# A hybrid GLA and RetNet decoder step: the input projection computed once for all tokens with seven products in place of eight, and spilled to DRAM

## The chip, the cores and the metric

The kernel runs on one core of a Trainium2 chip. The metric is device time in microseconds (us) of one execution. TensorE (PE) multiplies matrices, VectorE (DVE), ScalarE (ACT) and GpSimd (POOL) work elementwise, SyncE (SP) issues most transfers. Each engine runs its own instructions in order and waits on semaphores.

## The reference

One layer, for 1024 prompt tokens and 8 x 4 sample tokens (8 sequences that continue from stored states). All arithmetic is fp32.

```python
shift, scale, gate = split(c @ w_ada + b_ada)
h = x * (1 + scale) + shift
p = h @ w_in                      # 1024 -> 11280 columns
# GLA: q, k (4 heads x 128), v, z (4 x 256), low-rank forget input (16)
# RetNet: q, k (4 x 256), v, z (4 x 512); two merge gates of 1024
GLA:    S_t = diag(alpha_t) S_{t-1} + k_t^T v_t ; o_t = q_t S_t ; RMSNorm, * silu(z)
RetNet: rotary on q, k; S_t = gamma_h S_{t-1} + k_t^T v_t ; o_t = q_t S_t ; GroupNorm, * silu(z)
merged = sigmoid(mg) * (o_g @ w_branch_gla) + sigmoid(mr) * (o_r @ w_branch_ret)
y = LayerNorm(alpha * x + gate * (merged @ w_out))
```

Outputs are y and the final states of both branches, for prompt and sample.

## The kernel before, in words

**Precision.** A product of two fp32 matrices is made of three matmuls in the faster fp32r type: each operand is split into a high part (ScalarE copy, `split` L114, `wunit` L109) and a low part (VectorE subtraction, L115, L110), and hi x hi, lo x hi and hi x lo are summed in PSUM. So every block of 128 x 128 weights costs three matmuls. `wunit` loads 512 KB of weights and splits them.

**Halves.** The tokens are worked in two halves, `half(0)` with 512 prompt tokens and the 32 sample tokens, `half(1)` with the other 512. Each half runs the whole layer: `prep` makes h with channels on partitions, `ret_phase` goes through the four RetNet heads, `gla_phase` through the four GLA heads, `merge_phase` through the branches and gates, and the output projection and LayerNorm follow. All weights are read and split once in each half. States pass from half to half through DRAM.

**Projection.** `w_in` is not projected as a stage. Each head projects its own q and k (`proj_T`, `mm3`, L214 to L216: channels on PSUM partitions, 256, 288 or 512 tokens per matmul), its v (`v_units`, L246 to L248 and L253: tokens on partitions, 256 channels per matmul) and its z (`z_proj`), just before it needs them. `MR` and `MG` project the merge gates.

**Attention.** Both branches run in chunks of 128 tokens, four in each half. `A0` makes the masked scores of all chunks (L325, L664), `CPa`, `CPv` and `CP` split a chunk's operands, `C(c)` makes its output and updates the state S (L420, L738), `norm` normalises (with `rsqrt` on POOL, L124 and L125), `G(c)` transposes (L277), multiplies with silu(z) and splits. For sample tokens `ld(b)` or `SB` loads a stored state, `spl` splits it, `smm` multiplies and updates, and the new state is stored (L456, L471, L473, L475). `B(ob)` multiplies a head's result with the RetNet branch weights (L507 to L509) and adds into `acc`; `BG` does so for GLA (L850 to L852). `out_blk` is the output projection (L899 to L901).

**Order.** The order is written out by hand: `ret_phase` and `gla_phase` build a list `main`, in which the chunks of one head alternate with its z projections, the branch units of the head before, and q, k, v of the next head; `weave` spreads the sample units over it by the units' costs. The instructions of an engine are finally ordered when the program is built, by its own plan and not only in the order of this text.

Of the kernel before, what the change touches and what calls it, by code (L numbers as in the profile page):

```python
# [18 lines left out]
P = 128  # L19
# [4 lines left out]
NCH = 4  # L24
# [7 lines left out]
SUBOFF = (0, 32, 96, 192)  # L32


@with_exitstack
def hybrid_step(ctx: ExitStack, tc: tile.TileContext, a: dict):
# [21 lines left out]
    fold = ctile("fold", [64, 9], eng=nc.sync)  # L58
# [3 lines left out]
    def load_consts():  # L62
        rmask_s = ctile("rmask_s", [NS, HEADS, NS], eng=nc.sync)
        repsr = ctile("repsr", [P, HEADS], eng=nc.sync)
        repsr_s = ctile("repsr_s", [NS, HEADS], eng=nc.sync)
        rdw = ctile("rdw", [P, HEADS], eng=nc.sync)
        rdw_s = ctile("rdw_s", [NS, HEADS], eng=nc.sync)
        bmask_q = ctile("bmask_q", [P, 8, NS], eng=nc.sync)
        bmask_k = ctile("bmask_k", [P, 8], eng=nc.sync)
        scanm = ctile("scanm", [P, P + NS], eng=nc.sync)  # L70
        rg = ctile("rg", [P, 16], eng=nc.sync)
        gg = ctile("gg", [P, 8], eng=nc.sync)
        blr2 = ctile("blr2", [P, HEADS], eng=nc.sync)
        CC.__dict__.update(locals())

    def load_gmask():
        CC.gmask = const.tile([P, P], U8, name="gmask")
        CC.gmask_s = const.tile([NS, NS], U8, name="gmask_s")
        mtmp = wk.tile([P, 2, P], F32, tag="S0", name="mtmp", bufs=1)
        nc.gpsimd.dma_start(mtmp[:, 0, :], a["gmask"])  # L80
        nc.gpsimd.dma_start(mtmp[:NS, 1, :NS], a["gmask_s"])
        nc.vector.tensor_copy(CC.gmask, mtmp[:, 0, :])
        nc.vector.tensor_copy(CC.gmask_s, mtmp[:NS, 1, :NS])
# [3 lines left out]

    s_ret = [dp.tile([P, 2, DV_R], F32, name=f"sret{h}") for h in range(HEADS)]
    s_gla = [dp.tile([P, DV_G], F32, name=f"sgla{h}") for h in range(HEADS)]
    gate_d = dp.tile([2, P, 1024], F32, name="gate_d")  # L90

    def ps_mm():
        return psA.tile([P, 512], F32, tag="mm", name="mm")

    def ps_aux():
        return psA.tile([P, 512], F32, tag="aux", name="aux")

    def ps_o():
        return psC.tile([P, 512], F32, tag="o", name="o")

    def ps_so():
        return psC.tile([P, 512], F32, tag="so", name="so")

    def wunit(src, shape):
        raw = wp.tile(shape, F32, tag="raw", name="raw", bufs=2)
        nc.sync.dma_start(raw, src)
        wh = wp.tile(shape, F32R, tag="wh", name="wh")
        wl = wp.tile(shape, F32R, tag="wl", name="wl")
        nc.scalar.activation(wh, raw, AF.Copy)  # L109
        nc.vector.tensor_tensor(wl, raw, wh.bitcast(F32), op=sub)  # L110
        return wh, wl

    def split(hi, lo, src):
        nc.scalar.activation(hi, src, AF.Copy)  # L114
        nc.vector.tensor_tensor(lo, src, hi.bitcast(F32), op=sub)  # L115

    mhalf = const.tile([P, 1], F32, name="mhalf")
    nc.gpsimd.memset(mhalf, -0.5)

# [7 lines left out]
    def c_stack(t):  # L127
        nc.vector.tensor_scalar(t.rearrange("p k c -> p (k c)"), ident[:, 0:1].to_broadcast([P, KB * 64]), 0.0, None,
                                op0=mult)
        nc.scalar.activation(t[:, :, 0:9], cT, AF.Copy)  # L130
        nc.vector.tensor_tensor(t[:, :, 32:41], cT, t[:, :, 0:9].bitcast(F32), op=sub)
        return t

    def ada_fin(ps, kb):
        t = wk.tile([64, 256], F32, tag="on", name="mod", bufs=3)
        nc.scalar.activation(t, ps[:64, :256], AF.Copy)
        pt = ps[:, 256:274].rearrange("p (w c) -> p w c", w=2)
        for which in range(2):
            nc.tensor.matmul(pt[:, which, :], t[:, which * P:(which + 1) * P], fold, start=True, stop=True)
        nc.vector.tensor_tensor(modT[:, kb], pt, bada[:, :, kb:kb + 1].to_broadcast([P, 2, 9]), op=add)  # L140

    def gate_units(vj):
        Gt = SimpleNamespace()

        def begin():
            Gt.cT = c_stack(vj[:, 0, :].rearrange("p (k c) -> p k c", k=KB))
            Gt.sel = wk.tile([9, P + NS], F32, tag="rm", name="sel", bufs=1)
            nc.gpsimd.dma_start(Gt.sel, a["sel"])

        def col(j, kh):  # L150
            if kh == 0:
                Gt.ps = ps_mm()
            w = wunit(a["wgate"][2 * j + kh], [P, 4, 256])
            for k in range(4):
                for i in range(2):
                    nc.tensor.matmul(Gt.ps[:64, :256], Gt.cT[:, 4 * kh + k, :], w[i][:, k, :],
                                     start=kh + k + i == 0, stop=kh + k + i == 5)
            if kh == 1:
                g = wk.tile([P, TMAX], F32, tag="th", name="gn", bufs=3)[:9, :512].rearrange("p (i c) -> p i c", i=2)
                nc.gpsimd.dma_start(g[:, 0], a["bgate"][:, j * 256:(j + 1) * 256].partition_broadcast(9))  # L160
                nc.scalar.activation(g[:, 1], Gt.ps[32:41, :256], AF.Copy)
                nc.vector.tensor_tensor(g[:, 0], Gt.ps[:9, :256], g[:, 0], op=add)
                nc.vector.tensor_tensor(g[:, 0], g[:, 0], g[:, 1], op=add)
                Gt.g = g

        def spread(j):
            pm = ps_mm()
            for i, (c0, n) in enumerate(((0, P), (P, NS))):
                ps = pm[:n, i * 256:(i + 1) * 256]
                nc.tensor.matmul(ps, Gt.sel[:, c0:c0 + n], Gt.g[:, 0], start=True, stop=True)  # L170
                t = wk.tile([n, 256], F32, tag="on", name="gt", bufs=3)
                nc.scalar.activation(t, ps, AF.Copy, scale=0.5)
                nc.sync.dma_start(gate_d[i, :n, j * 256:(j + 1) * 256], t)

        L = [begin]
        for j in range(4):
            L += [lambda j=j: col(j, 0), lambda j=j: col(j, 1), lambda j=j: spread(j)]
        return L

    def half(hf):  # L180
        H = SimpleNamespace()
        T = TMAX if hf == 0 else TH
        groups = ((0, 256), (256, 544)) if hf == 0 else ((0, 512),)
        sample = hf == 0
        tb = [(c * P, P) for c in range(NCH)] + ([(TH, NS)] if sample else [])
        st_ = SimpleNamespace()
# [1120 lines left out]
```

## Time and profile before

| what | value |
|---|---|
| median of 3 runs | 1786.26 us (1785.05 to 1786.39) |
| profiled execution, span | 1784.8 us |
| PE busy | 1753.9 us (98%), 11724 matmuls |
| DVE busy | 1082.4 us (61%) |
| ACT busy | 797.8 us (45%) |
| POOL busy | 227.7 us (13%) |
| moved by DMA | 209.63 MB, 117 GB/s |

The profiled execution's own time, outside the profiler's span, is not given apart; its span is 1.5 us below the median of the runs. A row of a group reads: line, engine, operation, output<-inputs, shapes, count | busy us, mean ns of one | idle time of the engine before them, and what ended it. A row of a timeline reads: start, duration, engine, line, operation. A row of windows reads: stretch, its length, then busy time and count of PE, PEld (weight load), DVE, ACT, POOL, then the granted clock, the DMA share and GB/s. A row of waits reads: who waited for whom: us in total, times, longest.

### The profile page before, as it was taken

To read this page: it belongs to the slowest core of one execution; us is meant where nothing else is said; L and a number is where in the kernel's file an instruction comes from. 1 tells how busy PE (TensorE), PEld (TensorE's weight loads), DVE (VectorE), ACT (ScalarE), POOL (GpSimd) and SP (SyncE) were. 2 spreads that over 40 slices of the span, in tenths; PEclk is the share of its full clock that TensorE was granted. 3 is DMA by queue.
4 is the path that set the end of the run, shared out by engine and by line. 5 is a ranking of instruction groups with operands and counts; after the bars stand their busy time and mean duration, and the time that the engine had idled before them with its cause. 6 is when DMAs were issued, how large, how long until landed. Compare 5 with 4: busy or idle time off the path is not lost.

```text
span 1784.8 us, 29201 instructions
## 1 busy us (share of the span) xinstructions
PE 1753.9 (98%) x11724; PEld 1597.4 (90%) x11724; DVE 1082.4 (61%) x2065; ACT 797.8 (45%) x1463; POOL 227.7 (13%) x387
## 2 busy tenths in 40 slices
PE   7999999999999999999999999999999999999997
PEld 6999999999989999999999989888898888888887
DVE  5567467676588766655447765373645765544447
ACT  6453553453456555654224353432434644444320
POOL 3112011111120112112011000010000010001001
PEclk9999999999999999999999999999999999999999
DMA  7434343434452334434244422323232222222342
GB/s 281 137 124 162 121 152 120 142 130 136 142 178 95 108 93 147 126 101 148 94 161 129 135 71 97 97 94 95 62 115 73 87 79 71 84 83 86 95 165 83
DMA packets 62120, 209.63 MB, mean 117 GB/s; under 512 B 8883, under 2 KB 9856, under 8 KB 61984
## 3 DMA queue, kind: packets, MB, share of 16 engines
q1 hardware_dynamic: 44288, 146.50, 25.5%
q0 software_dynamic: 17696, 61.27, 10.2%
q8 instruction: 92, 1.51, 0.4%
q14 instruction: 44, 0.36, 0.1%
HBM read 176.54 MB, written 31.20 MB: 116 GB/s over the span
## 4 chain that ended last, share of the span: by engine, by line
PE 89%; DVE 4%; DMA 3%; ACT 1%; POOL 1%; issue 1%; SPq 0%; POOLq 0%; DVEq 0%; ACTq 0%
PE mm L214 13%; PE mm L215 13%; PE mm L216 13%; PE mm L246 5%; PE mm L247 5%; PE mm L248 5%; PE mm L507 3%; PE mm L508 3%; PE mm L509 3%; PE o L420 3%; PE aux L420 2%; PE mm L850 2%; PE mm L851 2%; PE mm L852 2%; PE aux L664 2%; DMA xt<-xT 2%
## 5 line engine op out<-in xcount | busy, mean ns | idle before, releaser
L214 PE MATMUL mm<-hh,wh 128*128 128x256 f32 (+2 forms) x1512 | 493.7, 328 | 0.7 <-POOL hh L207 0.5
L216 PE MATMUL mm<-hh,wl 128*128 128x256 f32 (+2 forms) x1512 | 490.4, 325 | 1.3 <-DVE wl L110 1.3
L215 PE MATMUL mm<-hl,wh 128*128 128x256 f32 (+2 forms) x1512 | 490.1, 324 | 0.9 <-DVE hl L208 0.9
L110 DVE TENSOR_TENSOR wl<-raw,wh 128x1024 fp32r<-128x1024 f32 x246 | 299.3, 1220 | 255.5 <-ACT wh L109 254.3
L109 ACT ACTIVATE wh<-raw 128x1024 fp32r<-128x1024 f32 x246 | 258.5, 1057 | 391.6 <-PE mm L215 219.9
L216 PEld LDWEIGHTS mm<-hh,wl 128*128 128x128 f32 x1512 | 286.3, 189 | 25.1 <-DVE wl L110 1.5
L215 PEld LDWEIGHTS mm<-hl,wh 128*128 128x128 f32 x1512 | 286.5, 189 | 23.1 <-DVE hl L208 1.4
L214 PEld LDWEIGHTS mm<-hh,wh 128*128 128x128 f32 x1512 | 285.6, 189 | 24.0 <-POOL hh L207 0.9
L246 PE MATMUL mm<-wh,hh 128*128 128x256 f32 x768 | 218.1, 284 | 0.0
L247 PE MATMUL mm<-wl,hh 128*128 128x256 f32 x768 | 216.4, 282 | 0.0
L248 PE MATMUL mm<-wh,hl 128*128 128x256 f32 x768 | 216.0, 281 | 0.0
L246 PEld LDWEIGHTS mm<-wh,hh 128*128 128x128 f32 x768 | 145.1, 189 | 1.1
L247 PEld LDWEIGHTS mm<-wl,hh 128*128 128x128 f32 x768 | 145.2, 189 | 0.5
L248 PEld LDWEIGHTS mm<-wh,hl 128*128 128x128 f32 x768 | 145.3, 189 | 0.0
L507 PE MATMUL mm<-oh,wh 128*128 128x288 f32 (+2 forms) x384 | 123.8, 323 | 0.0
L508 PE MATMUL mm<-ol,wh 128*128 128x288 f32 (+2 forms) x384 | 123.7, 322 | 0.0
L509 PE MATMUL mm<-oh,wl 128*128 128x288 f32 (+2 forms) x384 | 123.3, 321 | 0.0
L507 PEld LDWEIGHTS mm<-oh,wh 128*128 128x128 f32 x384 | 72.2, 188 | 5.8
L508 PEld LDWEIGHTS mm<-ol,wh 128*128 128x128 f32 x384 | 72.2, 188 | 5.3
L509 PEld LDWEIGHTS mm<-oh,wl 128*128 128x128 f32 x384 | 72.2, 188 | 5.1
L473 DVE SCALAR_TENSOR_TENSOR s0p<-s0p,aux 128x512 f32<-128x512 f32 x64 | 43.6, 682 | 45.0 <-PE aux L469 44.7
L899 PE MATMUL mm<-wh,mg 128*128 128x256 f32 x224 | 63.6, 286 | 2.6 <-ACT wh L109 1.6
(346 smaller groups left out, 3132.8 us busy)
## 6 DMA issues: line engine op xcount, KB each, us to landing
raw<-wqk_r SPq DMA_DIRECT2D x32, 512.0 KB, 3.7
s0p<-state_ret POOLq DMA_DIRECT2D x32, 512.0 KB, 4.2
raw<-wv_r SPq DMA_DIRECT2D x32, 512.0 KB, 3.6
raw<-wz_r SPq DMA_DIRECT2D x32, 512.0 KB, 3.6
o_srs<-s0p POOLq DMA_DIRECT2D x32, 512.0 KB, 3.4
raw<-wb_r SPq DMA_DIRECT2D x32, 512.0 KB, 3.6
raw<-wm SPq DMA_DIRECT2D x32, 512.0 KB, 3.5
stage<-wada SPq DMA_DIRECT2D x16, 512.0 KB, 7.5
```

The lines of the kernel that those rows point to most:

```text
L109: nc.scalar.activation(wh, raw, AF.Copy)
L110: nc.vector.tensor_tensor(wl, raw, wh.bitcast(F32), op=sub)
L214: nc.tensor.matmul(ps, w[0][:, k, cols], hh[:, k, g0:g1], start=k == 0, stop=False)
L215: nc.tensor.matmul(ps, w[0][:, k, cols], hl[:, k, g0:g1], start=False, stop=False)
L216: nc.tensor.matmul(ps, w[1][:, k, cols], hh[:, k, g0:g1], start=False, stop=k == KB - 1)
L246: nc.tensor.matmul(ps[:, :256], xh, wh[:, k % 4, :], start=k == 0, stop=False)
L247: nc.tensor.matmul(ps[:, :256], xh, wl[:, k % 4, :], start=False, stop=False)
L248: nc.tensor.matmul(ps[:, :256], xl, wh[:, k % 4, :], start=False, stop=k == KB - 1)
L420: nc.tensor.matmul(out, lhs(l), rhs(r), start=start and i == 0, stop=stop and i == 2)
L507: nc.tensor.matmul(ps, wh[:, j, cols], R.oh[:, j, g0:g1], start=j == 0, stop=False)
L508: nc.tensor.matmul(ps, wh[:, j, cols], R.ol[:, j, g0:g1], start=False, stop=False)
L509: nc.tensor.matmul(ps, wl[:, j, cols], R.oh[:, j, g0:g1], start=False, stop=j == 3)
```

## The change

The program becomes two stages, `project()` and `attend()`, each with its own buffers.

**Projection.** All 1056 tokens are projected together, as two sets of 528 (`HT`: 512 prompt and 16 sample tokens). One group is 256 columns of `w_in`, and its product is taken as 2 x 2 x 2 blocks: two token sets, two halves of the 1024 channels, two blocks of 128 columns. In place of the eight block products there are seven, of sums and differences of the blocks (a Winograd form of Strassen's scheme). The seven token operands (`XH`, `XL`, high and low) are made once, by `combos`; the four weight differences of each group are made by `tsum` on POOL, and `parts` splits each of the seven weight operands of 512 elements per partition. `step` runs one product as 2 x 12 matmuls of 264 tokens, `outs` recombines from PSUM. There are 44 groups. All results, v too, now have channels on partitions.

The post work of a group (`post_copy`, `post_z`, `post_rot`, `post_gla`, `post_m`) is run in portions within the next group's steps: rotary, the GLA decay products, silu, tanh. Its results are stored to DRAM tensors.

**Attention.** `attend()` reads them back by chunks (`ld`, `ldv`), and takes all eight chunks of a head in one go, so no state passes through DRAM. Order: GLA heads 0 and 1 (`gla_pair(0)`, with the gate columns woven in), four RetNet heads (`ret_stage`, with branch units: of the GLA pair beside head 0, of head h-1 beside head h), GLA heads 2 and 3 (`gla_pair(1)`, with the branch units of RetNet head 3), then the last branch units, the output projection in blocks of 512 columns, and LayerNorm. V is transposed on TensorE in `CP` and `CPv`. Several low parts move from DVE to POOL: those of queries, of GLA scores and of sample states (`spl`, `SB`). The branch products run in three groups of 352 tokens.

The diff, cut to its core:

```diff
-    h0, h1 = half(0), half(1)
...
+        def tsum(g, i):
+            r, T = G[g].raw, G[g].T
+            t = T[i] = wp.tile([P, 512], F32, tag="T", name="T", bufs=3)
+            x, y = {1: lambda: (r[:, 0, 1], r[:, 0, 0]), 2: lambda: (r[:, 1, 1], T[1]),
+                    3: lambda: (r[:, 1, 1], r[:, 0, 1]), 4: lambda: (r[:, 1, 0], T[2])}[i]()
+            nc.gpsimd.tensor_tensor(t, x, y, op=sub)
...
+        ORDER = ("P2", "P1", "P5", "P6", "P3", "P4", "P7")
...
+            split(wh.rearrange("p j c -> p (j c)"), wl.rearrange("p j c -> p (j c)"), right(g, p))
...
+            for j in js:
+                for i, (w, x) in enumerate(((wh, xh), (wh, xl), (wl, xh))):
+                    nc.tensor.matmul(ps[:, :SUB], w[:, j, :], x[:, j, c], start=start and j == 0 and i == 0,
+                                     stop=stop and j == 3 and i == 2, skip_group_check=True)
...
+        def combos(j):
+            h0, h1 = xs[j], xs[j + 4]
+            S, S_ = st("S12"), st("S34")
...
+            nc.vector.tensor_tensor(S[:, 0], h0[:, 1], h1[:, 1], op=add)
+            sp(4, S[:, 0])
+            nc.vector.tensor_tensor(S[:, 1], S[:, 0], h0[:, 0], op=sub)
+            sp(5, S[:, 1])
...
+            emit_parts(n + AHEAD)
...
+                step(g, i)
+            for _ in range(rate[0]):
+                if todo:
+                    todo.pop(0)()
+            if i == 6:
+                while todo:
+                    todo.pop(0)()
+                todo += plan[g][2](G[g])
+                if g + 2 < NG:
+                    load_raw(g + 2)
...
+            def CPv(c):
+                v = R.vz[c][0]
+                pv = ps_aux()
+                for j in range(4):
+                    nc.tensor.transpose(pv[:, j * P:(j + 1) * P], v[:, j, :], ident)
+                vj = R.vj[c] = wk.tile([P, 2, DV_R], F32R, tag="vj", name="vj", bufs=1)
+                split(vj[:, 0], vj[:, 1], pv)
...
+            def SPl():
+                s = R.s12 = wk.tile([P, 12, NS], F32, tag="s12", name="s12")
+                for j in range(4):
+                    for o, src in ((0, qk_d), (4, v_d), (8, z_d)):
+                        nc.gpsimd.dma_start(s[:, o + j].rearrange("p (h t) -> p h t", h=2), src[h][:, j, :, TH:])
...
+            def spl(b, d):
+                R.ar = wk.tile([P, 2, DV_R], F32R, tag="ar", name="ar")
+                split(R.ar[:, 0], R.ar[:, 1], R.sb[b][0][:, d, :], nc.gpsimd)
...
+            for c in range(NCH):
+                main.append((3.4, lambda c=c: C(c)))
...
+            weave(main, samp, fill)
...
+        og0 = gla_pair(0, gate_units)
...
+            fill = branch(4, og0[0], og0[1], fin_g0)
+            for h in range(HEADS):
+                oh, ol = o4("oh"), o4("ol")
+                ret_stage(h, oh, ol, wk, fill)
+                if h < 3:
+                    fill = branch(h, oh, ol, fin_r(h))
...
+        og1 = gla_pair(1, fill_r3)
...
+    project()
+    attend()
```

More of the change, by code (lines that the diff above doesn't have):

```diff
@@ L101, in ps_so @@
[L101 to L115, printed above, removed]
+    dec = const.tile([P, HEADS, 16], F32, name="dec")
@@ L125, in rsqrt @@
         nc.gpsimd.tensor_tensor(out, out, mhalf[:n], op=ALU.pow)
[L127 to L178, printed above, removed]
@@ L390, in open_s @@
[L390 to L397 removed]
+                v = R.vz[c][0]
+                pv = ps_aux()
+                for j in range(4):
+                    nc.tensor.transpose(pv[:, j * P:(j + 1) * P], v[:, j, :], ident)
@@ new lines, in ret_stage @@
+            samp = [S0, lambda: ldb(0), lambda: ldb(1)]
+            for b in range(8):
+                for d in range(2):
+                    samp += [lambda b=b, d=d: spl(b, d), lambda b=b, d=d: smm(b, d)]
+                if b + 2 < 8:
+                    samp.append(lambda b=b: ldb(b + 2))
+            samp += [SF, SG]
+            for f in (lambda: ld(0), lambda: ldv(0), SPl, lambda: ld(1), lambda: ldv(1), lambda: A0(0), SP,
+                      lambda: CPa(0), lambda: CPv(0)):
+                f()
@@ L510, in B @@
                     if h == 0:
-                        nc.scalar.activation(st_.acc[:, ob, g0:g1], ps, AF.Copy)
+                        nc.scalar.activation(A, ps, AF.Copy)
                     else:
-                        nc.vector.tensor_tensor(st_.acc[:, ob, g0:g1], ps, st_.acc[:, ob, g0:g1], op=add)
-            R.qku = cost(5.3, [lambda w=w, g=g: qk(w, g) for w in range(2) for g in range(len(groups))])
-            R.open, R.qkf, R.A0, R.SP, R.open_v, R.open_att = open_, qk, A0, SP, open_v, open_att
@@ L929, in out_ln @@
                 nc.sync.dma_start(dst[:, cs], yh)
-        H.__dict__.update({k: v for k, v in locals().items() if callable(v)})
-        H.groups, H.tb, H.sample, H.st = groups, tb, sample, st_
-        return H
-    def cost(w, units):
-        for u in units:
-            u.w = w
-        return units
-    def weave(main, extra):
-        ws = [getattr(u, "w", 0.3) for u in main]
-        n, m, i, done = sum(ws), len(extra), 0, 0.0
-        for u, w in zip(main, ws):
+        seq = [8] + list(range(8))
@@ L944, in weave @@
+        for c in seq:
+            xld(0, c)
+        for c in seq:
+            blk(0, c)
+        xld(1, seq[0])
+        for n, c in enumerate(seq):
+            if n + 1 < 9:
+                xld(1, seq[n + 1])
+            blk(1, c)
+            ln(c)
+    def weave(main, extra, fill):
+        total = sum(w for w, _ in main) or 1.0
+        ne, nf = len(extra), len(fill)
+        ie = jf = 0
+        done = 0.0
+        for w, u in main:
             u()
             done += w
-            while i < m and (i + 1) * n <= done * m + 1e-6:
-                extra[i]()
-                i += 1
@@ L1163, in hybrid_step @@
[L1163 to L1178 removed]
+            while jf < nf and (jf + 0.5) * total <= done * nf + 1e-6:
+                fill[jf]()
+                jf += 1
@@ L1181, in _constants @@
+            while ie < ne and (ie + 1) * total <= done * ne + 1e-6:
+                extra[ie]()
+                ie += 1
+        for u in extra[ie:]:
+            u()
+        for u in fill[jf:]:
+            u()
+    project()
+    attend()
 def _constants():
```

1784 lines of the change are left out of this document (925 added, 859 removed).

## The prediction

> **What bounds the kernel now.** I read the engine shares first, then the chain that ended last, then rows of single matmuls.
>
> ```profile
> span 1784.8 us, 29201 instructions
> PE 1753.9 (98%) x11724; PEld 1597.4 (90%) x11724; DVE 1082.4 (61%) x2065; ACT 797.8 (45%) x1463; POOL 227.7 (13%) x387
> PE 89%; DVE 4%; DMA 3%; ACT 1%; POOL 1%; issue 1%; SPq 0%; POOLq 0%; DVEq 0%; ACTq 0%
> ```
>
> TensorE is busy 98% of the span and carries 89% of the chain; no other engine comes near. But a busy matmul row overlaps its neighbours, so the price of one is the distance between starts. In the timeline (start, duration, engine, line):
>
> ```profile
> 900.04 0.28 PE L214 MATMUL mm<-hh,wh 128*128 128x256 f32 x1
> ...
> 902.06 0.28 PE L216 MATMUL mm<-hh,wl 128*128 128x256 f32 x1
> 902.18 0.29 PE L214 MATMUL mm<-hh,wh 128*128 128x288 f32 x1
> ...
> 905.23 0.29 PE L216 MATMUL mm<-hh,wl 128*128 128x288 f32 x1
> ...
> 1177.89 0.39 PE L214 MATMUL mm<-hh,wh 128*128 128x512 f32 x1
> ...
> 1180.40 0.39 PE L216 MATMUL mm<-hh,wl 128*128 128x512 f32 x1
> 1180.63 0.60 PE L277 MATMUL aux<-c_ident,on 128*128 128x128 f32 x4
> 1180.99 1.64 PE L420 MATMUL aux<-vj,kn 128*128 128x512 f32 x6
> ```
>
> Between the first two rows lie 17 starts: 0.119 us for 256 columns. 23 starts in the next pair give 0.133 us for 288, 11 starts 0.228 us for 512. Interpolated: 0.122 us at 264 columns, 0.160 at 352. The price falls nearly with the columns, so fewer columns is less time. Four transposes take 0.36 us, 0.09 each.
>
> **The projection.** Groups by line and shape:
>
> ```profile
> L246 PE MATMUL mm<-wh,hh 128*128 128x256 f32 x768 | 218.1, 284 | 0.0
> L214 PE MATMUL mm<-hh,wh 128*128 128x512 f32 x512 | 205.4, 401 | 0.0
> L214 PE MATMUL mm<-hh,wh 128*128 128x288 f32 x496 | 146.4, 295 | 0.5 <-POOL hh L207 0.5
> L214 PE MATMUL mm<-hh,wh 128*128 128x256 f32 x504 | 142.5, 285 | 0.2
> L899 PE MATMUL mm<-wh,mg 128*128 128x256 f32 x224 | 63.6, 286 | 2.6 <-ACT wh L109 1.6
> ```
>
> L214 has two equal companions (L215, L216), L246 has L247 and L248. Before: 3 x (512 x 0.228 + 496 x 0.133 + 504 x 0.119) = 728 us, 2304 V matmuls x 0.119 = 274, the sample rows of V (L253, 192) 23, the first head's parts that went to other PSUM tiles (72) 9: 1034 us. After: 44 groups x 7 products x 2 halves x 12 = 7392 matmuls of 264 columns x 0.122 = 904 us. **Gain 130 us.**
>
> The other TensorE terms: out_blk in 512 columns instead of 256, 768 x 0.119 against 384 x 0.228: -4. Branches: the same columns in three groups of 352, nil. V now arrives with channels on partitions, so 216 new transposes x 0.09: +19. The forget gate's input, 80 matmuls instead of 48 (the second token set needs three terms): +2. Two more prices by the timeline:
>
> ```profile
> 14.59 0.61 PE L139 MATMUL aux<-c_fold,mod 64*128 64x9 f32 x4 [0.21 <-ACT mod L136]
> 649.88 3.74 PE L664 MATMUL aux<-GZ,kh 128*32 128x32 f32 x32
> ```
>
> The adaLN matmuls become 128 plain fp32 of 9 columns, each two rows (as L139's two matmuls show four): 256 x 0.15 = 38 us at most. I cost them at nothing, since they lie in the start beside some 48 us of transfers (below); with that cover gone they would add 16 us over today's 144 x 0.119 and 32 x 0.15. A0 of one head and half (L664) takes 3.7 us, as before. Net -113 us.
>
> **What covers what in the first stage.** One group is 168 x 0.122 = 20.5 us of TensorE.
>
> ```profile
> L110 DVE TENSOR_TENSOR wl<-raw,wh 128x1024 fp32r<-128x1024 f32 x246 | 299.3, 1220 | 255.5 <-ACT wh L109 254.3
> L115 DVE TENSOR_TENSOR Sx<-S,Sx 128x512 fp32r<-128x512 f32 x48 | 31.1, 686 | 2.4 <-ACT Sx L114 2.0
> L513 DVE TENSOR_TENSOR acc<-mm,acc 128x288 f32<-128x288 f32 x24 | 10.9, 455 | 10.2 <-PE mm L509 10.1
> L114 ACT ACTIVATE ar<-s0p 128x512 fp32r<-128x512 f32 x64 | 40.1, 627 | 33.0 <-DMA s0p<-state_ret 14.2 <-PE so L471 6.4 <-DVE ar L115 5.9
> L573 POOL MEMSET AT<- 128x512 f32 x2 | 1.1, 529 | 4.0 <-PE o L420 4.0
> ```
>
> Posts are priced by elements, 0.69 us for 512 on VectorE and 0.63 on ScalarE. VectorE per group: 7 weight splits x 0.69 + 8 recombinations of 264 columns x 0.43 = 8.2 us; the rotary post adds 6.7, the GLA post about 7: at most 15 of 20.5. ScalarE: 7 x 0.63 + 8 x 0.4, plus 5 in z groups: 12.6. POOL gets four subtractions of 512 (new there): one lies between 0.53 us (the memset, which only writes) and 1.6 (three such streams); I take 1.1, 4.4 us a group. Only the four GLA groups, whose post has some 16 us on POOL, come near 20.5. Nil while TensorE sets the pace; cover gone, up to 2 us in each of these four. Per group 1 MB is read and 1.1 MB spilled through SP, 102 GB/s; over the run the spill and its reading add about 115 MB and the second reading of the weights (63 MB) goes, so 210 becomes about 262 MB, 150 GB/s.
>
> ```profile
> 0.00:50.00 50.00, 39.41 (x258) 32.98 (x259) 26.35 (x34) 30.46 (x40) 18.06 (x35) 1.00 0.78 285
> 50.00:100.00 50.00, 48.29 (x393) 47.17 (x392) 28.09 (x59) 22.89 (x42) 3.24 (x9) 1.00 0.35 109
> ```
>
> The start moved 285 GB/s (last column), so 150 is nil. Its own length is bytes: w_ada 8.4 MB, both token halves 4.3, the first weights 1, at 285 GB/s 48 us, then one set of splits; before, one half (2.2) and 1.6 MB of weights: 43. **+5 us.**
>
> **What lost its cover: the attention.** Before, every chunk had projections beside it. Now GLA pair 0 has only the gate columns as fill, each RetNet head eight branch units, pair 1 eight more. In pair 0 ScalarE is the bound:
>
> ```profile
> L114 ACT ACTIVATE vjg<-GV 128x256 fp32r<-128x256 f32 x32 | 13.2, 413 | 0.3
> L114 ACT ACTIVATE xS<-AT 128x128 fp32r<-128x128 f32 x32 | 9.8, 305 | 0.0
> L719 ACT ACTIVATE on<-o,ssq 128x256 f32<-128x256 f32 x32 | 15.2, 475 | 31.9 <-POOL ssq L125 31.9
> L717 ACT ACTIVATE on<-o 128x256 f32<-128x256 f32 x32 | 12.1, 379 | 5.1 <-DMA gate_d<-gt 4.2 <-PE o L738 0.9
> L772 ACT ACTIVATE kst<-kdr,c_bmask_k 128x128 fp32r<-128x128 f32 x32 | 11.3, 393 | 2.1 <-DVE kdr L228 2.1
> L109 ACT ACTIVATE wh<-raw 128x1024 fp32r<-128x1024 f32 x246 | 258.5, 1057 | 391.6 <-PE mm L215 219.9 <-PE mm L508 66.0 <-PE mm L851 25.5
> ```
>
> A chunk costs it three splits of 256 (0.41 each), two of 128 (0.305), Square with its 0.2 read-out, and the scaled copy: 2.9 us, x 16 = 46. Samples 16 x 0.39 + 8 x 0.63 = 11, gate weights 8 x 1.06 = 8.5, the rest (set-up, A0's split) 13: 79 us. TensorE has there 16 chunks x 9 x 0.119, samples 6, A0 15, transposes 7, gates 8: 53. With ScalarE filled to 85% the pair takes 93: **+40 us**. In pair 1, with branch work, TensorE has 89 and VectorE about 90 (60 of the pair, 24 x 1.06 of the merge, 5 of weights); two engines that full seldom mesh, I take 104: **+15**. In a RetNet head TensorE has 96 us (26 chunk matmuls, 46 branch, 11 samples, the rest transposes and scores) and VectorE 90 (per chunk 6.7, per sample batch 1.6, per branch unit 2.2, by 0.69 for 512 wide and about 0.42 for 256): **+4 each, +16**. The nearest row is the window where VectorE was 85% busy and TensorE still full (nothing lost); the other bound is a tenth, 10 each:
>
> ```profile
> 550.00:600.00 50.00, 50.00 (x402) 48.84 (x401) 42.63 (x111) 31.05 (x51) 0.12 (x1) 1.00 0.28 85
> L320 POOL DMA_DIRECT2D rm<-rmask x8 | 4.6, 570 | 51.5 <-DVE Af L327 50.0 <-PE mm L170 1.6
> ```
>
> Between the stages the last group's post, its store, fresh loads of 3 to 4 us and one score and split set stand alone: **+12**. At heads' borders 12 small sample loads go through POOL (0.57 us each by the last row); branch units cover them, 7 us each where not.
>
> The sum: 1784.8 - 113 + 5 + 40 + 15 + 16 + 12 = 1760, against a span of 1784.8; the median of the runs is 1.5 above it: **1761 us**. The 80 us that TensorE was not filled before (1785 less 1705 by these prices) are left in.
>
> **A rule against the change.** The splits' low parts of queries, scores and sample states move from VectorE to POOL. In the trace POOL has almost no elementwise work (13% busy, much of it issue). The Trainium skill, GPSIMD Engine Reference, sections 3.1 and Key points, says that a two-input operation takes POOL about twice VectorE's time and that POOL contends with VectorE instructions that have two SBUF inputs; by it a 512-wide one is an estimated 1.35 us and the third rival's 1846 would be about 1865. No row here shows it.
>
> **Rivals.** (1) TensorE stays fed: units are moved across chunks. For it: the build does not keep the order of the text. In the code A0's L664 stands wholly before the first Z's L214; in the trace:
>
> ```profile
> 590.60 0.30 PE L664 MATMUL aux<-GZ,kh 128*64 128x32 f32 x2
> 590.83 0.33 PE L673 MATMUL aux<-c_ident,KE 128*128 128x128 f32 x1
> 590.91 0.37 PE L214 MATMUL mm<-hh,wh 128*128 128x256 f32 x1
> 591.12 0.28 PE L664 MATMUL aux<-GZ,kh 128*96 128x32 f32 x2
> ```
>
> Against: pair 0 has too little to move. 1784.8 - 113 + 5 + 12 + 1.5 = 1690.
>
> (2) Slower by one wait: POOL's queue in the RetNet samples. ldb's load waits until the store from that buffer has landed, and the split's low part, now on POOL, stands behind it; smm on TensorE waits for that, and behind smm the next chunk. By waits and POOL's timeline:
>
> ```profile
> POOL s0p L456 <- DMA o_srs<-s0p: 59.9, 21, 5.7
> 503.00 0.73 POOL L475 DMA_DIRECT2D o_srs<-s0p  x1 [1.16 <-DVE qp L458]
> 509.46 0.72 POOL L456 DMA_DIRECT2D s0p<-state_ret  x1 [5.72 <-DMA o_srs<-s0p]
> ```
>
> The wait exists (21 times, 2.9 us mean); before, only rsqrt stood behind it. Store, landing and load take 3 to 6.5 us and the low part 1.1: some 5 us a batch, and by the woven order 20 of 32 batches have no branch unit in between: 1761 + 100 = 1861. It decides from 25 us on, 0.8 us a batch. Against: the moved order above.
>
> (3) POOL and VectorE exclude each other: per RetNet head POOL gets 16 x 1.1 + 7 x 0.6 = 22 us, VectorE 90 + 22 = 112, so +12 each; the pairs' 19 us on top of 90 and 71 add 22 and 13: 1761 + 85 = 1846.
>
> (4) The seven products give no gain, were a start bound by its weight load; the three prices by columns speak against it.
>
> **How the numbers follow.** Less than 0.2% can't be told from no change here. Forecast 0.50, between 1722 (the uncovered terms halved) and 1790; rival 1 0.12; rival 2 0.22; rival 3 0.13; no change by mixture 0.03. The range reaches to 1700 and 1870: below lies most of rival 1, above part of rival 2. Faster 0.60 (forecast less 0.02, and rival 1), same 0.05, slower 0.35. The forecast's own range is 1722 to 1790.
>
> **What would show it.** Right: 7392 projection matmuls spaced 0.12 us, ending near 970 us; pair 0 some 90 us long with ScalarE over 80% busy; RetNet heads about 100 us with VectorE near 90%. Wrong: TensorE waiting on POOL's ar in the samples (rival 2), VectorE's 512-wide subtractions longer than 0.69 us (rival 3), or gaps in the first stage behind POOL's subtractions.

## The result, and the profile after

The changed kernel takes 1978.91 us (1972.42 to 1982.17), the kernel before beside it 1786.33: a ratio of 1.108 [1.105, 1.110], 193 us slower. The prediction said 1761 us and faster. Since e5 below shows the seven products to be worth 133 us, everything else in the change costs about 326 (193 + 133).

The page of the changed kernel: its shares, TensorE's busy time and clock in 40 slices, and the chain by engine:

```profile
span 1970.6 us, 31563 instructions
PE 1768.3 (90%) x11944; PEld 1636.0 (83%) x11944; DVE 1138.1 (58%) x2120; ACT 825.2 (42%) x1695; POOL 747.5 (38%) x899
PE   7899888999999999999997878889898997876796
PEclk9999999999999999999997779999999999897898
PE 65%; DMA 11%; POOL 10%; DVE 6%; ACT 5%; issue 4%; SPq 0%; POOLq 0%; DVEq 0%; ACTq 0%
```

TensorE falls from 98 to 90% of a longer span and from 89 to 65% of the chain. POOL's busy time triples. Cut at the borders of the stages (columns as in the windows of before):

```profile
0.00:100.00 100.00, 80.16 (x368) 76.95 (x369) 38.51 (x63) 33.15 (x52) 21.87 (x44) 1.00 0.47 163
100.00:360.00 260.00, 233.99 (x1850) 228.80 (x1849) 154.14 (x287) 133.50 (x249) 109.83 (x123) 0.97 0.34 112
360.00:1031.30 671.30, 671.30 (x5532) 671.21 (x5530) 350.23 (x575) 289.04 (x564) 196.50 (x145) 1.00 0.30 105
1031.30:1054.80 23.50, 10.97 (x62) 9.02 (x60) 8.86 (x22) 7.71 (x15) 12.79 (x20) 0.64 0.76 231
1054.80:1157.80 103.00, 84.35 (x468) 67.73 (x468) 64.80 (x160) 61.09 (x188) 61.43 (x102) 0.78 0.56 172
1157.80:1288.00 130.20, 107.81 (x562) 89.83 (x563) 87.29 (x163) 53.90 (x101) 60.22 (x75) 0.92 0.73 219
1288.00:1402.00 114.00, 105.66 (x581) 90.15 (x581) 74.37 (x140) 62.26 (x121) 57.99 (x73) 0.98 0.53 156
1402.00:1517.00 115.00, 102.50 (x567) 86.61 (x566) 80.92 (x157) 51.45 (x95) 53.91 (x68) 0.99 0.51 148
1517.00:1635.00 118.00, 107.75 (x586) 92.56 (x587) 84.07 (x166) 51.86 (x96) 53.42 (x69) 0.96 0.44 131
1635.00:1758.00 123.00, 106.53 (x705) 95.62 (x703) 82.13 (x208) 59.85 (x184) 63.33 (x107) 0.94 0.57 171
1758.00:1856.00 98.00, 60.58 (x269) 52.12 (x269) 40.94 (x74) 16.68 (x28) 30.18 (x39) 0.83 0.41 122
1856.00:1970.60 114.60, 96.73 (x412) 75.42 (x410) 71.86 (x112) 4.68 (x7) 26.08 (x41) 0.93 0.29 99
```

These are, in order: the start; the GLA groups of the projection; its other groups; the border; GLA pair 0; the four RetNet heads; pair 1; the last branch units; the output. The third row is what the change is for: 5532 matmuls in 671.30 us, 0.1213 us each, with TensorE never idle. No other row is like it.

| stage | predicted us | measured us | more |
|---|---|---|---|
| projection, start included | 970 | 1031.3 | 61 |
| border | 12 | 23.5 | 11 |
| GLA pair 0 | 93 | 103 | 10 |
| four RetNet heads | 400 | 477.2 | 77 |
| GLA pair 1 | 104 | 123 | 19 |
| last branch units and output (what is left of 1760) | 181 | 212.6 | 32 |
| sum | 1760 | 1970.6 | 210 |

TensorE's waits from the border to the output (who waits for whom: us in total, times, longest) name four places:

```profile
PE mm L661 <- DVE thl L1208: 36.2, 20, 4.3
PE aux L996 <- ACT on L960: 15.1, 4, 4.0
PE so L1060 <- POOL ar L93: 14.4, 20, 1.3
PE mm L1122 <- DVE cstk L1112: 9.1, 1, 9.1
```

The first is the last branch units, the second the ends of the four heads, the third the sample states' low parts on POOL, the fourth the border, where the gate columns' operand is late.

### The profile page after: what moved, and what is told of

It is laid out like the page before. It is cut to its first block, busy times and chain, and to the rows that moved or that the text cites. A ratio compares the mean times of both kernels' runs of the same rounds, so it can differ in the third digit from the quotient of the medians.

```text
span 1970.6 us, 31563 instructions
## 1 busy us (share of the span) xinstructions
PE 1768.3 (90%) x11944; PEld 1636.0 (83%) x11944; DVE 1138.1 (58%) x2120; ACT 825.2 (42%) x1695; POOL 747.5 (38%) x899
## 4 chain that ended last, share of the span: by engine, by line
PE 65%; DMA 11%; POOL 10%; DVE 6%; ACT 5%; issue 4%; SPq 0%; POOLq 0%; DVEq 0%; ACTq 0%
PE psA L157 18%; PE psC L157 12%; PE psD L157 6%; PE psB L157 6%; DMA thl<-m0d 3%; PE o L647 3%; PE mm L661 2%; PE mm L662 2%; PE mm L663 2%; PE aux L647 2%; PE psada L495 2%; PE aux L709 2%; POOL ar L93 1%; POOL acc L1207 1%; POOL kh L408 1%
## 5 line engine op out<-in xcount | busy, mean ns | idle before, releaser
L157 PE MATMUL psA<-xh,wh 128*128 128x264 f32 x1056 | 301.8, 286 | 6.8 <-ACT C L193 6.8
L157 PE MATMUL psA<-xl,wh 128*128 128x264 f32 x1056 | 301.0, 285 | 0.8 <-DVE xl L93 0.8
L157 PE MATMUL psA<-xh,wl 128*128 128x264 f32 x1056 | 300.9, 285 | 0.0
L157 PE MATMUL psC<-xh,wh 128*128 128x264 f32 x704 | 202.2, 288 | 9.7 <-ACT xh L92 7.0
L157 PEld LDWEIGHTS psA<-xh,wh 128*128 128x128 f32 x1056 | 199.4, 189 | 7.7 <-ACT C L193 7.6
L157 PE MATMUL psC<-xl,wh 128*128 128x264 f32 x704 | 201.3, 286 | 0.0
L157 PEld LDWEIGHTS psA<-xl,wh 128*128 128x128 f32 x1056 | 199.7, 189 | 1.7 <-DVE xl L93 1.7
L157 PE MATMUL psC<-xh,wl 128*128 128x264 f32 x704 | 201.1, 286 | 0.0
L157 PEld LDWEIGHTS psA<-xh,wl 128*128 128x128 f32 x1056 | 199.9, 189 | 0.0
L93 DVE TENSOR_TENSOR wl<-raw,wh 128x512 fp32r<-128x512 f32 (+1 forms) x164 | 144.9, 890 | 90.9 <-ACT wh L92 90.6
L157 PEld LDWEIGHTS psC<-xl,wh 128*128 128x128 f32 x704 | 133.5, 190 | 0.8 <-DVE xl L93 0.7
```

Source lines behind the costliest of these rows:

```text
L93: (eng or nc.vector).tensor_tensor(lo, src, hi.bitcast(F32), op=sub)
L157: nc.tensor.matmul(ps[:, :SUB], w[:, j, :], x[:, j, c], start=start and j == 0 and i == 0, stop=stop and j == 3 and i == 2, skip_group_che ...
```

## The experiments

Ratios are to the kernel before on the same chip, to be read against 1.108 [1.105, 1.110] of the change as it was.

### What the seven products are worth

**e5: an eighth product.** `prod` runs P3 once more into D's PSUM in each group, and P4, which belongs there, overwrites it.

```diff
                     q.b["D", s] = bank("BD", 3, "psD")
+                    prod(g, "P3", s, q.b["D", s], True, True)
```

> The changed kernel with an eighth product in each group (24 more matmuls of 264 columns into a PSUM bank that the next product overwrites; 1056 matmuls in all, outputs unchanged). It measures what the seventh part less is worth. Theory A (TensorE sets the pace of the first stage): +1056 x 0.121 = 128 us, less what the four GLA groups and the start hide, so +110 to +130, about 2095. Rival C (the seven products are paced by the splits, the recombination or POOL's differences, so that the saved product bought little): +0 to +60.

2112.46 us, ratio 1.183 [1.180, 1.186]: +133.5 for 1056 matmuls more, 0.126 us each and just above the range. The saved product is paid out in full; the loss is elsewhere.

### The start

The chain of the start, in order of time (start, length, what):

```profile
1.64 3.83 DMA ada<-wada
5.61 13.80 PE psada L495 x64
19.43 0.19 DVE modT L497
...
20.30 1.25 ACT xt L507
...
23.50 1.78 DVE xl L93
...
28.29 6.64 PE psada L495 x32
```

adaLN's rows take 13.80 / 64 = 0.216 us each, 256 of them 55 us, and each block's sums and splits stand behind its adaLN.

The 0.216 us is a slow clock, though the windows read 1.00 for this stretch. The matmuls of 264 columns that lie between the adaLN blocks start 0.22 us apart up to 95.5 us, and from there 0.12 us apart (TensorE's timeline):

```profile
94.19 0.42 PE L157 MATMUL psC<-xh,wl 128*128 128x264 f32 x1
94.42 0.42 PE L157 MATMUL psC<-xl,wh 128*128 128x264 f32 x1
...
96.82 0.28 PE L157 MATMUL psA<-xl,wh 128*128 128x264 f32 x1
96.94 0.28 PE L157 MATMUL psA<-xh,wl 128*128 128x264 f32 x1
```

Their weight loads take 0.33 us in the first part and 0.19 in the second, as they do on the two sides of the head's end shown further down, where the granted clock reads 0.50 and then 1.00. An adaLN row at the full rate stands in e10 (below), right where its matmuls of 264 columns turn from 0.22 to 0.14 us apart; eight rows take 0.95 us, 0.12 each:

```profile
21.94 0.95 PE L491 MATMUL psada<-c_cT,c_ident 128*128 128x9 f32 x8
```

**e2: adaLN with moving weights.** fp32r, 256 columns moving, hence 32 splits of w_ada on ScalarE and VectorE.

```diff
-                    nc.tensor.matmul(pt[:, w, :], raws[kb][k // 4][:, k % 4, w * P:(w + 1) * P], cT[:, k, :], ...
+                split(wh, wl, raws[kb][q // 2][:, 2 * (q % 2):2 * (q % 2) + 2, :])
...
+                        nc.tensor.matmul(ps[:64, :256], cs[:, 2 * q + k, :], w[:, k, :], ...
```

> The changed kernel, with the adaLN parameters computed as before the change: c stationary (high and low part stacked), 256 columns of weights moving, a fold, instead of 128 plain fp32 matmuls of 9 columns that need 256 weight loads. Theory A: those 256 rows stood 0.2 us apart on the path of the first 100 us; now 128 rows and 32 of the fold, so the first stage's full rate begins near 65 us instead of 98, whole about 1945. Rival B (the start is set by the 13.7 MB of transfers, as my prediction had it, 48 us plus splits): the start does not move by more than 5 us.

1972.34 us, 1.105 [1.102, 1.108]: not distinguishable from no change. VectorE's work in the first 100 us rose from 38.5 to 63.3 us, ScalarE's from 33.2 to 56.1.

From this I concluded that adaLN is not the start's limit. That was wrong, as the next runs show. Why this form gains nothing has two candidates that are not told apart: the splits of w_ada load the engines that the tokens' sums and splits need, and TensorE again runs at the slow rate up to 91.5 us, but for 51 to 64 us.

**e7: no loads of w_ada; e11: a quarter of adaLN's matmuls; e10: both.**

```diff
 e7, e10:
-                nc.sync.dma_start(r, a["wada"][2 * kb + kh])
-   ... matmul(pt[:, w, :], raws[kb][k // 4][...], cT[:, k, :]
+   ... matmul(pt[:, w, :], ident, cT[:, k, :]
 e10, e11:
-                for k in range(KB):
+                for k in (0, 4):
```

> The sixteen loads of w_ada are left out; the 128 adaLN matmuls read the identity instead, so their number and shape stay and the modulation's values differ. Theory C (the start is a chain: loads go out two at a time as the nine buffers of st come free, some 19 us a pair, and TensorE, fed in pieces, runs at half rate until 98 us): without those loads six of the ring's turns are gone, and the full rate begins near 60 us: -30 to -45 us. Rival D (the start is TensorE's and VectorE's own work, adaLN, modulation and sums in order, at half rate): -0 to -10 us.

> The loads of w_ada are left out as before and of adaLN's 128 matmuls only a quarter is left (two of eight k steps, on the identity), so the modulation's values differ. Without the loads alone the time did not move, and the chain then ran over adaLN's matmuls (0.216 us for each of 256 rows, 56 us of the first 83). Theory C2 (the start has two chains of the same length side by side, the loads and adaLN on TensorE, and taking one leaves the other): with both gone the full rate begins near 55 us, -30 to -45 us. Rival (x's loads, sums and splits hold the start): 0 to -15 us.

> The loads of w_ada stay and adaLN has a quarter of its matmuls (two of eight k steps; the values differ). Theory C2: the loads' chain is left, -5 to -15 us, as adaLN with moving weights gave -6.6. Rival (adaLN on TensorE alone is the start's chain): -30 to -45 us, as much as with the loads gone too.

e7: 1976.59 us, 1.108 [1.105, 1.111], nothing. e11: 1946.73, 1.090 [1.086, 1.094], -32. e10: 1932.17, 1.082 [1.080, 1.085], -47. In e7 theory C fell and its rival D held. e10 came out just past its range, but e11 is as its rival said, so theory C2, two chains of the same length, fell too. adaLN on TensorE is the start's chain: taking 8 MB of transfers away gains nothing while it stands, taking three quarters of it away gains 32 with all the transfers in place, and the loads are worth 15 more only behind it. In e7's chain of the first 110 us adaLN's rows have 44.1%.

**e13: e2 with the low parts on POOL.**

```diff
-                split(wh, wl, raws[kb][q // 2][:, 2 * (q % 2):2 * (q % 2) + 2, :])
+                split(wh, wl, raws[kb][q // 2][:, 2 * (q % 2):2 * (q % 2) + 2, :], nc.gpsimd)
```

> adaLN with the weights moving (fp32r, 256 columns, as in the earlier run that gave -6.6) and their low parts on POOL instead of VectorE. If VectorE's and ScalarE's splits were what that form paid with: -15 to -25 us against the changed kernel. If POOL's 1.3 to 1.45 us for each of 32 low parts (about 44 us) takes their place in the chain, or the loads hold the start: 0 to -8 us.

1979.67 us, 1.107 [1.103, 1.111]: nothing. Relieving VectorE alone does not help; the slow rate lasts up to 96.4 us here, and again the splits and the clock are not told apart.

**e14: plain fp32 with the nine columns as weights and w_ada moving, unsplit.**

```diff
+                nc.tensor.matmul(ps[:9, :256], cT[:, k, :], raws[kb][k // 4][:, k % 4, :], start=k == 0, stop=k == KB - 1)
+            nc.scalar.activation(t, ps[:9, :256], AF.Copy)
...
+                nc.tensor.matmul(pt[:, w, :], t[:, w * P:(w + 1) * P], ident[:9, :9], start=True, stop=True)
```

> adaLN in plain fp32 with the nine columns as weights and w_ada moving, 64 matmuls of 256 columns instead of 128 of nine, with no splits; the result is turned by 16 small matmuls. A plain fp32 matmul of 256 columns took some 0.6 to 1.0 us in the gate spread, two rows: 64 x 0.62 = 40 us at the better rate against 56 us. If adaLN on TensorE is the start's chain: -8 to -18 us. If the moving rows run at the worse rate (64 x 1.0 = 64 us): 0 to +8 us.

1953.90 us, 1.091 [1.089, 1.094]: -25, above the range expected. In the tile's rows (duration min/median/max in ns), the first two of the changed kernel, the others of e14:

```profile
L495 PEld LDWEIGHTS psada<-c_cT,ada x256: 285/333/337, 5.6 to 87.9; 128*128 128x128 f32 x128
L495 PE MATMUL psada<-c_cT,ada x256: 216/362/363, 5.6 to 87.9; 128*128 128x9 f32 x128
```

```profile
L494 PEld LDWEIGHTS psada<-ada,c_cT x128: 86/91/141, 5.8 to 61.7; 128*9 128x9 f32 x128
L494 PE MATMUL psada<-ada,c_cT x128: 379/379/634, 5.8 to 61.9; 128*9 128x256 f32 x128
```

The weight load shrinks from 333 to 91 ns, there are half as many rows, and adaLN's last row starts at 61.9 us in place of 87.9. The clock has a part in this: e14's rows start 0.43 us apart up to 10.9 us and 0.22 from there. How much of the 25 us is the form and how much the clock is not told apart.

Over all these runs the gain follows the time from which the 264-column matmuls keep starting 0.12 us apart:

| run | full rate from, us | time less that of the changed kernel, us |
|---|---|---|
| changed kernel | 95.9 | 0 |
| e13 | 97.3 | +1 |
| e2 | 91.9 | -7 |
| e7 | 90.7 | -2 |
| e14 | 72.4 | -25 |
| e11 | 69.4 | -32 |
| e10 | 52.7 | -47 |

### The GLA groups of the projection

**e3: kh's subtractions on VectorE instead of POOL (L408).**

```diff
-                        nc.gpsimd.tensor_tensor(F[:, t], dch(t)[:, :, 32 * i + 15...
+                        nc.vector.tensor_tensor(F[:, t], dch(t)[:, :, 32 * i + 15...
```

> The changed kernel, with the eight subtractions of the decayed GLA keys (kh) of each GLA group on VectorE instead of POOL (7 us of POOL's time a group, 4 groups). Theory A: between 150 and 350 us TensorE waits for the forget-gate's next part behind a chain POOL, ScalarE, VectorE; with POOL relieved most of the 33 us that are lost there come back, whole about 1950 to 1960. Rival B (VectorE is then the full engine, 15 + 3.4 us and its waits): nothing gained, within 8 us of 1979.

1965.94 us, 1.101 [1.096, 1.106], -13: less than the 19 to 29 expected, and the interval slightly overlaps that of the changed kernel. TensorE's wait behind that chain (who for whom: us in total, times, longest), in the changed kernel and in e3:

```profile
PE psg L318 <- DVE D L320: 16.1, 3, 5.4
```

```profile
PE psg L318 <- DVE D L320: 4.7, 3, 2.6
```

The wait shrinks by 11 us, which bears the gain out. At 0.1213 us each the 1850 matmuls of this stretch are 224 of its 260 us, so about a third of the 36 lost was POOL's chain; the rest was not taken apart.

### The attention without its cover

**e4: all low parts of the attention back on VectorE; e4b: only ar's.**

```diff
 e4 and e4b:
-                split(R.ar[:, 0], R.ar[:, 1], R.sb[b][0][:, d, :], nc.gpsimd)
+                split(R.ar[:, 0], R.ar[:, 1], R.sb[b][0][:, d, :])
 e4, besides:
-                    split(x[:, 2], x[:, 3], R.A[t][:, c % 4, :], nc.gpsimd)
+                    split(x[:, 2], x[:, 3], R.A[t][:, c % 4, :])
 ... and so for R.qt, the sample states sr, and qs
```

> All low parts that the change put on POOL in the attention (GLA scores and queries, sample states, RetNet queries, ar) go back to VectorE; the first stage is left as it is. Theory A (the stages without cover are held by their own chains; POOL costs only the waits that name it, about 28 us of ar and a few of srg, and VectorE gets 16 x 0.69 + 7 x 0.7 = 16 us more work per RetNet head in return): 1979 to 1950, that is 0 to -30 us. Rivals 2 and 3 of the prediction (POOL's queue in the samples, or POOL and VectorE excluding each other, are where the heads' time went): -60 to -100 us, the heads back near 100 us each.

> Only ar, the 512-wide low part of each RetNet sample state, goes back to VectorE. Theory A: the 28 us of waits for ar shrink to about a third, VectorE gets 64 x 0.7 = 45 us more over four heads in which it is 65 to 75% busy: -10 to -20 us. If VectorE is the bound of a head: 0 to +20. Rival 2: nearly all that the full return of the low parts gives, -60 or more.

e4: 1979.83 us, 1.109 [1.106, 1.112], nothing. e4b: 1966.49, 1.102 [1.098, 1.106], -12 as expected, with an interval that slightly overlaps that of the changed kernel. So having ar on POOL costs some 12 us, and handing the other low parts back to VectorE as well loses as much again. Rivals 2 and 3 of the prediction, 60 to 100 us here, fall as causes of the heads' length.

**e9: 32 units of 8 extra matmuls of 512 columns in GLA pair 0; e9r: 16 extra matmuls of 352 columns behind each branch unit of the RetNet heads.**

```diff
 e9:
+            def more():
+                ps = ps_mm()
+                for k in range(8):
+                    nc.tensor.matmul(ps[:64, :], Gt.cT[:, k, :], Gt.cT.rearrange("p k c -> p (k c)"), ...
+            return [begin] + [f for u in L[1:] for f in (u, more, more)] + [more] * 8
 e9r, in branch(), for u not in (3, 5):
+                    for r in range(2):
+                        ps = ps_mm()[:, :352]
+                        for j in range(8):
+                            nc.tensor.matmul(ps, wh[:, j % 4, cols], oh[:, j % 4, :352], ...
```

> GLA pair 0 gets 32 extra units of 8 matmuls of 512 columns, woven between the gate units and read by nobody: 256 x 0.228 = 58 us of TensorE at the full rate. Theory A (the pair, 103 us, is held by chains of small steps, TensorE has room and its matmuls there run slower than full rate for want of work): the time rises by 0 to 25 us, and the pair's other matmuls are closer together. Rival (TensorE, busy 84 of the 103 us, is itself the bound of the pair): +50 us or more.

> Each branch unit of the four RetNet heads is followed by 16 extra matmuls of 352 columns read by nobody: 8 x 16 x 0.16 = 20.5 us of TensorE per head, 82 us in all. Theory A (a head of 114 to 130 us holds 96 us of TensorE's work and some 20 us of stalls that nothing fills): the extra work fills part of the stalls, +40 to +65 us. Rival (TensorE is the bound of the heads and the stalls are gone wherever it has work ready): +75 to +90 us.

e9: 2003.75 us, 1.123 [1.120, 1.126], +25 for 58 us of matmuls. Pair 0, from its first gate column to the first score of RetNet head 0, first in the changed kernel and then in e9:

```profile
1040.50:1157.80 117.30, 95.20 (x527) 76.76 (x527) 69.47 (x174) 65.33 (x198) 72.10 (x117) 0.76 0.59 180
```

```profile
1042.00:1186.20 144.20, 137.30 (x778) 99.54 (x778) 69.49 (x174) 66.84 (x198) 67.76 (x117) 0.92 0.48 147
```

The granted clock rises from 0.76 to 0.92, and a gate matmul takes 279 ns at the median in place of 415 (one row each of the tile, the changed kernel's first):

```profile
L1122 PE MATMUL mm<-wh,cstk x32: 277/415/562, 1040.5 to 1123.8; 128*64 128x256 f32 x32
```

```profile
L1122 PE MATMUL mm<-wh,cstk x32: 275/279/443, 1042.0 to 1145.3; 128*64 128x256 f32 x32
```

Pair 0 has room on TensorE, and what runs there runs dearer for want of work: "busy 95 of 117" overstates its load. ScalarE is busy 65 of 117 us (56%), so it is not the bound either, and neither VectorE (69) nor POOL (72) is full. By elimination the pair is held by its chains of small dependent steps; the chain itself was not followed.

e9r: 2059.74 us, 1.155 [1.151, 1.158], +81 for 82 us. My theory fell here and its rival held. Work put behind the branch units costs its full price: where TensorE has branch work, it is already the bound. e12 looks for the stalls where no unit is left.

**e12: the last branch unit of a head kept for the head's end.**

```diff
-            main.append((0.4, lambda: G(NCH - 1)))
-            weave(main, samp, fill)
+            weave(main, samp[:-1], fill[:-1])
+            fill[-1]()
+            G(NCH - 1)
+            SG()
```

> In each RetNet head the last branch unit is kept until the last chunk's steps and the samples' sum have been issued, and the last gate steps come after it. Theory A (at a head's end TensorE waits some 4 us for the norm of the last rows and then runs at half rate for 1 to 2 us, because the branch units are used up before): the four waits go, -12 to -22 us. Rival (the order of the build decides, not the order of the text, or the stall moves into the next head's first scores): within 4 us.

1967.94 us, 1.101 [1.097, 1.105], -11, just under the range. At the end of head 0, TensorE's timeline of the changed kernel (start, duration, operation, and in brackets the idle time before it), then of e12:

```profile
1285.31 0.63 PE L996 MATMUL aux<-c_ident,on 32*128 32x32 f32 x4 [4.04 <-ACT on L960]
...
1288.33 0.49 PE L662 MATMUL mm<-ol,wh 128*128 128x352 f32 x1
1288.63 0.49 PE L663 MATMUL mm<-oh,wl 128*128 128x352 f32 x1
...
1291.05 0.33 PE L662 MATMUL mm<-ol,wh 128*128 128x352 f32 x1
1291.21 0.32 PE L663 MATMUL mm<-oh,wl 128*128 128x352 f32 x1
```

```profile
1279.76 0.43 PE L996 MATMUL aux<-c_ident,on 32*128 32x32 f32 x4 [0.38 <-ACT on L960]
...
1281.28 0.32 PE L662 MATMUL mm<-ol,wh 128*128 128x352 f32 x1
1281.44 0.32 PE L663 MATMUL mm<-oh,wl 128*128 128x352 f32 x1
```

After a wait of 4 us the same matmul starts every 0.30 us; 2.7 us later every 0.16. With the wait at 0.4 us it is 0.16 at once.

### The last branch units and the output

**e1: m0 in buffers of its own.** `th` and `m0` share the two buffers of `thl`, so each group of 352 tokens waits for a load, POOL's sum and VectorE's sum, one after the other. The chain of waits there, in the changed kernel:

```profile
1767.04 3.68 DMA thl<-m0d
...
1770.79 0.94 POOL acc L1207
...
1771.76 0.54 DVE acc L1209
...
1772.31 2.85 DMA thl<-m0d
```

```diff
-            m0 = load_th(mp, 0, ob, g0, g1, m0_d)
+            m0 = mp.tile([P, 512], F32, tag="y1", name="m0l", bufs=2)[:, :352]
+            nc.sync.dma_start(m0, m0_d[:, ob, g0:g1])
```

> The changed kernel, with one edit: in the last branch stage the gate (th) and the stored first part (m0) of a 352-token group no longer share two buffers; m0 gets two of its own, so the loads run one group further ahead. Theory A (the loss is made of waits that lost their cover; here a load of 2.3 us, an addition on POOL of 0.95 and one on VectorE of 0.54 follow one another, 3.8 us for each of 24 groups against 1.9 us of matmuls): the stage falls from 98 to about 55-65 us and the whole from 1979 to about 1940. Rival B (the stage is slow because POOL's or VectorE's own work is too long, or the transfers' bandwidth is used up): the two loads stay 3 to 4 us apart, the stage stays near 95 and the whole within 10 us of 1979.

1947.13 us, 1.090 [1.088, 1.093], -32 of some 39 expected. The mechanism holds, but only half of the wait went: 36.2 us became 17.9, and the stage is 72 us long, not 55 to 65.

**e6: two more buffers for y1.**

```diff
-            y = ys[i, c] = y0[:, c] if i == 0 else mp.tile([P, 512], F32, tag="y1", name="y1", bufs=2)
+            y = ys[i, c] = y0[:, c] if i == 0 else (mp.tile(...) if c % 2 else
+                wp.tile([P, 512], F32, tag="raw", name="y1", bufs=2))
```

> The output's chunks y1 get two more buffers (every other one in the idle buffers of raw). Theory A (the tail waits for the load of x_prompt's rows into a buffer that the previous chunk frees, about 3 us four times): -8 to -12 us. Rival (the tail is held by the store of y or by the last operations of VectorE): within 3 us.

1974.49 us, 1.106 [1.103, 1.109], -4: less than expected and not distinguishable from no change. The load left the chain, and LayerNorm's chain on VectorE and POOL, 5.6 us a row block, took its place.

### All repairs together

> Four repairs together, each measured alone: m0 in buffers of its own (-32), the first-stage low parts kh on VectorE (-13), y1 in four buffers (-4), ar on VectorE (-12): by the sum 1918 us. If they share waits, 1930. It stays slower than before in either case.

> The four repairs and the last branch unit at the head's end (-11 alone): 1914.5 - 11 = 1903 us; 1914 if its stall was already covered by ar on VectorE.

> The five repairs and adaLN in plain fp32 with moving weights: 1903 less whatever the adaLN form gives alone, 1890 to 1908 us.

b1 (e1, e3, e4b, e6): 1914.51 us, 1.072 [1.067, 1.077]. b2 (with e12): 1894.89, 1.060 [1.056, 1.064]. b3 (with e14): 1871.66, 1.045 [1.042, 1.048], lower than its range. The gains add: 107 us in all against 98 by the single runs. More than half of the 193 is won back, and the kernel still takes 4.5% longer than the one before. Its projection ends at 995.5 us, pair 1 takes 109, the last units 70, the output 105.5. The border with pair 0, and the heads:

```profile
995.50:1121.50 126.00, 94.97 (x518) 77.62 (x518) 73.96 (x181) 68.86 (x202) 70.27 (x115) 0.74 0.58 177
1121.50:1586.00 464.50, 429.82 (x2383) 368.61 (x2382) 352.76 (x705) 218.81 (x419) 154.67 (x240) 0.96 0.59 178
```

The border and pair 0 are 126 us, as they were (126.5), and the heads 116 each. Against the forecast of 105 and 400 these two are 86 of the 110 us that b3's span of 1870.5 is still above 1760.

## Why the prediction was wrong, point by point

The mechanism forecast for the projection's arithmetic held. What failed are the terms for nearly everything else:

- **The projection's gain, right.** 0.122 us for 264 columns was forecast, 0.1213 measured, and e5 puts the saved product at 133 us. (7392 x 0.122 is 902, not 904: 2 us more gain, of no weight.)
- **adaLN "at nothing", wrong; with the last branch units the largest error that a single run shows.** The step named the cover (48 us of transfers) and 16 us if it were gone. Both failed. A row took 0.216 us instead of 0.15 (55 us against "38 at most"): the row of 0.15, at 14.59 us of the kernel before, has neighbours of 256 columns that start 0.12 us apart soon after, so it was a price near the full rate, and the changed kernel's start runs at about half of it until 95.5 us. And adaLN does not lie beside the transfers but between them and the splits, in series. e11 puts three quarters of it at 32 us, e7 shows that the transfers hide nothing. Hidden work has to be independent of what hides it.
- **The GLA groups' POOL work "nil", wrong.** Forecast up to 2 us in each of four groups if the cover went; e3 alone gives 13 us. The sum per engine (16 of 20.5 us) was no measure for a chain that passes POOL, ScalarE and VectorE before the next product may start.
- **Border +12, wrong by 11.** 9.1 us of it is one wait for the gate columns' operand (L1112).
- **Pair 0 at 93 us bound by ScalarE "over 80% busy", wrong in its mechanism.** 103 us with ScalarE 59% busy; e9 shows TensorE with room. Adding up ScalarE's work gave nearly the right length for the wrong reason.
- **RetNet heads +4 each, wrong by 77 us in sum.** The row "85% busy, nothing lost" came from a window in which TensorE had 192 branch matmuls and 144 of the next projections to run. Here VectorE is only 65 to 71% busy, so "near 90%" failed too. Two causes were shown: ar on POOL (12 us, e4b) and the heads' ends with the slow restart behind them (11 us, e12). e9r shows that the rest is not a lack of work between the branch units. With both repaired b3's heads are only 13 us shorter and still take 464.5 us against the 400 forecast. The windows say where the rest lies: the forecast had 96 us of TensorE's work in a head, 384 in all, and 16 us without it. Measured, TensorE is busy 423.7 of 477.2 us in the changed kernel and 429.8 of 464.5 in b3. So the term for TensorE's own work is some 40 us too small, and in b3 it is most of what is left. The granted clock of 0.92 to 0.99 in the heads is part of it; why the work is dearer beyond that stays open.
- **Pair 1 at 104, measured 123.** Not tested alone; with the repairs it is 109.
- **The last branch units, missed.** No term of the sum looked at what the merge waits for once it has no attention beside it. Two buffers shared by two loads cost 32 us (e1).
- **Rivals.** 1 falls with the stages above, 4 with e5. 2's wait is there, at 12 us instead of 100. 3 falls: the 512-wide subtraction on VectorE takes 698 ns, against 686 before, with POOL three times as busy:

```profile
L93 DVE TENSOR_TENSOR wl<-T,wh 128x512 fp32r<-128x512 f32 x176 | 122.4, 698 | 165.0 <-ACT wh L92 161.6
L134 POOL TENSOR_TENSOR T<-raw 128x512 f32<-128x512 f32 x88 | 114.7, 1304 | 326.7 <-DVE wl L93 257.8 <-issue 68.1 <-POOL T L134 0.7
```

The second row is POOL's two-input operation: 1.30 us, not the 1.1 that I took (`ar` takes 1.35, the other form of `T` 1.45). The estimate of 1.35 us from the Trainium skill, GPSIMD Engine Reference, sections 3.1 and Key points, agrees; that page's contention does not show in the first row. The slower side came in by a way that no rival named: several terms, most of them costed as covered when the change had taken their cover away. Six repairs of such terms give 107 of the 193 us; the rest, above all pair 0 and the heads, is located but not explained.

## What to carry to other kernels

The account that fits these runs: the main engine was 98% busy because independent work stood beside its chains; the change gathered that work into one dense stage, gained its arithmetic there and uncovered the chains elsewhere. Price each remaining stage by its longest chain of dependent steps and its buffers, not only by the sum per engine, and ask of each step costed at nil whether it needs what is said to hide it. A removed cost that shows no gain (e7) may stand behind another: take out each alone and both together (e7, e11, e10) before calling either free. And take the price of a matmul from a row that ran at the rate which the new stage will have.

## What the hardware showed

- After a wait of some 4 us TensorE ran at half its rate for a few us. By windows of the changed kernel's first head end:

```profile
1285.30:1290.40 5.10, 5.09 (x22) 5.03 (x23) 2.01 (x6) 1.30 (x4) 3.82 (x7) 0.50 0.64 167
1290.40:1294.70 4.30, 4.30 (x28) 4.30 (x28) 0.72 (x3) 1.08 (x3) 4.30 (x7) 1.00 0.25 23
```

  The clock is 0.50 for 5.1 us after the wait and 1.00 behind. The Trainium skill, TensorE: Matmul & The Clock Gate, section on the HAM clock gate, puts the cold clock at 1.2 GHz and the time to warm up at about 3.4 us of sustained work; 352 columns at 1.2 GHz are an estimated 0.293 us, and the trace's 0.30 agrees; the 5.1 us here are longer than the page's 3.4. So a stall of 4 us in a dense stretch costs more than 4 us, and e9's pair 0 shows the other side: added work makes its neighbours cheaper.
- What TensorE is given decides whether the full rate comes. In the changed kernel 13.8 us of nine-column rows back to back (5.6 to 19.4 us) did not bring it; in e14 the full rate came after 5.1 us of rows of 256 columns (5.8 to 10.9 us).
- A plain fp32 row of nine columns against 128 x 128 weights cost 0.216 us at the slow rate and 0.12 at the full one (e10), as much as 264 columns of fp32r at either rate. Turned round, with the nine columns as weights, the whole kernel took 25 us less.
- The granted clock read 1.00 over the first 100 us while the 264-column matmuls started 0.22 us apart: the spacing of known matmuls is the safer sign.
